# A later transposition of differences and of memory keys, and a softmax scaling that changes its engine

## The chip, the cores and the metric

The kernel runs on one core of one Trainium2 chip. The metric is the device time of one execution in microseconds (us). A core has TensorE (PE: products and transpositions; PEld are its weight loads), VectorE (DVE), ScalarE (ACT), GpSimd (POOL), SyncE (SP, which only issues transfers) and 16 DMA engines. Each engine does its own instructions in the order in which they were written; between engines there are only semaphores.

## The reference

Two layers of an encoder on 512 tokens of 1024 features, all in fp32. Layer 0 mixes tokens by dilated windows (8 heads, three dilations), layer 1 by grouped attention (8 query heads, 2 heads of keys and values). Both layers also attend to 256 memory tokens with 4 heads. The outputs are gated, projected and added to the residual stream:

```python
for i in range(DEPTH):
    h = rmsnorm(x, norm_g[i])
    mem_h = rmsnorm(mem, mem_norm_g[i])
    proj = jnp.einsum('bsd,de->bse', h, w_in_a[j])      # layer 1: w_in_b
    o_mix = mixer_dilated(qkv, ...)                     # layer 1: mixer_axial_gqa(q, k, v, ...)
    o_mem = memory_attention(q_mem, mem_h, w_mem_kv[i], mem_qn_g[i], mem_kn_g[i])
    y = jnp.concatenate([o_mix, o_mem], axis=-1) * jax.nn.silu(gate)
    x = x + jnp.einsum('bse,ed->bsd', y, w_out[i])

def memory_attention(q_mem, mem_h, w_kv, qn_g, kn_g):
    q = rmsnorm(q_mem, qn_g) * (HEAD_DIM ** -0.5)
    kv = mem_h @ w_kv                                   # keys (normed by heads) and values
    p = jax.nn.softmax(jnp.einsum('bqhe,bkhe->bhqk', q, k), axis=-1)
    return jnp.einsum('bhqk,bkhe->bqhe', p, v)
```

The grouped attention of layer 1 has the same softmax, over 512 keys.

## The kernel before

**Operands in two parts.** Each fp32 operand of a product is split into a high part (`wh`, or the first of a pair; a cast, mostly on ScalarE) and a low part (`wo`, the rest; a subtraction on VectorE). A product is then three matmuls, high by high, high by low and low by high: lines 163 to 165, `mm3`. For weights the cast is L285 and the subtraction L295.

**Products by Strassen's way.** The large projections (`s_chunk`, L352) use seven products instead of eight, and these need differences of halves of the rows and of the features. For layer 1 they are made from the rows that leave the first output projection. `ev_o` (L1187) takes one block b of 128 rows of the new x after the other: it stores it to DRAM, norms it, and for b = 2 and 3 calls `sum_h` (L504: S1, one subtraction on VectorE), waits `EO[2]` groups, and calls `sums_h` (L509), which transposes S1 (`put_h`: four transpositions into a bank `xT` on TensorE, then the split into `hS`, L157 and L160) and makes three more differences (L514 to L516). `rest_h` then transposes the others (S2, S4, S3, 22), one kind in each group. The tiles of the differences are called `xs` in the profile.

**Groups.** The `Driver` (L41) writes all engines' programs together. After each group of products (12 of 512 columns or 24 of 256) its `tick` lets every waiting generator do one step: `yield n` means go on after n groups. What is given to `drv.late` is written at the end of the tick, what is given to `drv.soon` at the start of the next. So a step's place in each engine's program is fixed by the number of groups, not by time. Where the program of TensorE has a transposition, its products behind it wait until the operand is there.

**Memory keys and values.** `mem_kv` (L593) projects the memory tokens in each layer, 48 products for keys and 48 for values. `ev_k` norms the keys (squares on ScalarE, `rstd` on GpSimd, the product `xn` on VectorE, L534), transposes them on TensorE (`qT`, L541) and splits them with their gain (`kmT`, L589 and L590). `ev_v` splits the values (`vm`, L607 and L609). In layer 1 this lies between the output projection of layer 0 and the first chunk of layer 1, right where `ev_o` ends. The products' banks `pj` are four, used in turn, so a bank of keys or values must be read before a later chunk writes it.

**Attention.** `mem_attn` (L629) and `attn_b` (L1314) are pipelines of steps over pieces of 256 queries (memory) or one head and 128 queries (grouped). In step t TensorE makes the scores of piece t (`sm`, `sb`), VectorE the row maximum (`top`, written late), ScalarE the exponentials of piece t - 1 with their row sums, VectorE for piece t - 2 the reciprocal of the row sum and the scaling of the probabilities by it and by 0.5 (L655; L1336), TensorE the transposition of piece t - 3 (`pmt`, `ptb`), ScalarE and VectorE its high and low part (`pmT`, `pbT`), and TensorE the product of piece t - 4 with the values (`om`, `ob`). The 0.5 belongs to the gate, which is made as t (1 + tanh(t / 2)). In layer 1 the probabilities `pb` take their tiles from the pool of 512-wide tiles that also holds the outputs `o` on their way to DRAM and `og` on their way back to the gates.

**GpSimd and the weights.** Sums of weight quarters are made by transfers that add (GpSimd issues them, lines 247 to 269). Its program also has the tables of layer 1 (L1223), which wait for `grB` on VectorE (L1220).

Of the kernel before, what the change touches and what calls it, by code (L numbers as in the profile page):

```python
# [10 lines left out]
F32 = mybir.dt.float32  # L11
F32R = mybir.dt.float32r
AF = mybir.ActivationFunctionType
ALU = mybir.AluOpType
# [12 lines left out]
MEM_STEP = 1, 1  # L27
MEM_D = 4
PD, W_EARLY = 1, True
EO = 1, 2, 1, 1, 1  # L30
YB = {"m": (2, 2), "k": (1, 1, 1), 0: (1, 2, 1), 1: (1, 2, 1)}
Y = [3, 2, 2, 2, 3, 2, 2, 1, 1, 1]

# [91 lines left out]
def trunk_kernel(ctx: ExitStack, tc: tile.TileContext, x, mem, wall, norm_g, mem_norm_g, gcol,  # L125
                 qn_a, kn_a, qn_b, kn_b, ident_d, mask_d, tab_a, tab_b, out):
    nc = tc.nc
    V, A, G, T = nc.vector, nc.scalar, nc.gpsimd, nc.tensor
# [14 lines left out]
    def s2(dt=F32, name="s2"):  # L143
        return pool.tile([128, 512], dt, tag="s2", name=name, bufs=NS2)
# [7 lines left out]
    def sm(n, name):  # L152
        return small.tile([128, n], F32, tag="sm%d" % n, name=name)
# [439 lines left out]
    def mem_kv(layer, M):  # L593
        kt_ = [m4(F32R, "kmT").rearrange("p (h t) -> p h t", h=4) for _ in range(2)]
        vt_ = [m4(F32R, "vm").rearrange("p (b e) -> p b e", b=2) for _ in range(2)]

        def ev_k(b, p):
            r = head_sq(p)
            yield 1
            xn = head_mul(p, r)  # L600
            yield 1
            q = transpose4(xn)
            cs = slice(b * 128, (b + 1) * 128)
            yield from put_norm(q, gk_m[layer], kt_[0][:, :, cs], kt_[1][:, :, cs])

        def ev_v(b, p):
            A.copy(vt_[0][:, b], p)  # L607
            yield 1
            V.tensor_tensor(vt_[1][:, b], p, vt_[0][:, b].bitcast(F32), ALU.subtract)  # L609

        proj_t(M, NAT[:2], ev_k)
        proj_t(M, NAT[:2], ev_v)
        return kt_, vt_
# [15 lines left out]
    def mem_attn(qm, km, vm, put, step):  # L629
# [8 lines left out]
                mm3(sp[:, j, :], qm[h // 2][0][:, h % 2, cs], qm[h // 2][1][:, h % 2, cs], km[0][:, h, :], km[1][:, h, :], True, True)  # L638

        def top(i):  # L640
            pr[i] = (sm(2, "nmm"), sm(2, "denm"), s2(name="pm").rearrange("p (b k) -> p b k", b=2))
            V.tensor_reduce(pr[i][0], sc[i], axis=AX.X, op=ALU.max, negate=True)

        def exps(i):
            nm, den, pp = pr[i]
            sp = sc.pop(i)
            for j in range(2):
                A.activation(pp[:, j], sp[:, j], AF.Exp, bias=nm[:, j:j + 1], accum_out=den[:, j:j + 1])

        def scale(i):  # L650
            _, den, pp = pr[i]
            rd = sm(2, "rdm")
            V.reciprocal(rd, den)
            for j in range(2):
                V.tensor_scalar(pp[:, j], pp[:, j], rd[:, j:j + 1], 0.5, ALU.mult, ALU.mult)  # L655

        def turn(i):
            pp = pr.pop(i)[2]
# [23 lines left out]
        def out_(i):  # L682
            h, b2 = divmod(i, 2)
            if b2:
# [2 lines left out]
                put(h, os)  # L687

        yield from pipeline(8, (0, score, 0), (4, pv, 0), (3, turn, 0), (2, scale, 0), (1, exps, 0),
                            (0, top, 1), (3, hi, 1), (3, lo, 1), (4, out_, 1), step=step)  # L690

    def out_rest(ys, acc, done, evac):

# [605 lines left out]
    def ev_kv(q, u, t):  # L1299
        i, j = int(q[0]) - 1, int(q[1]) - 1  # L1300
        if j:
            hi, lo = [v[:, 2 * i:2 * i + 2] for v in vb]
            tv = t.rearrange("p (b e) -> p b e", b=2)
            A.copy(hi, tv)
            yield 1
            V.tensor_tensor(lo, tv, hi.bitcast(F32), ALU.subtract)
# [7 lines left out]
    def attn_b():  # L1314
# [7 lines left out]
            mm3(sc[i], qh[h % 4 // 2][:, h % 2, cs], ql[h % 4 // 2][:, h % 2, cs], kbT[0][:, h // 4], kbT[1][:, h // 4], True, True)  # L1322

        def top(i):
            pr[i] = sm(1, "nmb"), sm(1, "denb"), s2(name="pb")
            V.tensor_reduce(pr[i][0], sc[i], axis=AX.X, op=ALU.max, negate=True)

        def exps(i):
            nm, den, pp = pr[i]
            A.activation(pp, sc.pop(i), AF.Exp, bias=nm, accum_out=den)  # L1330

        def scale(i):
            _, den, pp = pr[i]
            rd = sm(1, "rdb")
            V.reciprocal(rd, den)
            V.tensor_scalar(pp, pp, rd, 0.5, ALU.mult, ALU.mult)  # L1336

        def turn(i):
            b2, j = divmod(i, 2)
            pp = pr.pop(i)[2]  # L1340
            if j == 0:
                pts[b2] = [m4(F32R, "pbT").rearrange("p (k q) -> p k q", k=4) for _ in range(2)]
            tp[i] = at("ptb").rearrange("p (k q) -> p k q", k=4)
            for k in range(4):
                T.transpose(tp[i][:, k, :], pp[:, k * 128:(k + 1) * 128], ident)  # L1345
# [19 lines left out]
        def out_(i):  # L1365
# [5 lines left out]
            if b == 3:  # L1371
                put_ob(h, rs[h])

        yield from pipeline(32, (0, score, 0), (4, pv, 0), (3, turn, 0), (2, scale, 0), (1, exps, 0),
                            (0, top, 1), (3, hi, 1), (3, lo, 1), (4, out_, 1),
                            ready=lambda i: n_rot[0] >= 8 + i // 16 * 4)

    for kvh in range(2):
# [134 lines left out]
```

## Time and profile before

| | |
|---|---|
| median of 3 runs | 983.4 us (982.01 to 985.52) |
| profiled execution: its time | 983.15 us |
| profiled execution: its span, first to last instruction | 981.4 us |
| mean granted clock of TensorE | 0.995 |
| transpositions of differences, L471 | 48 instructions, TensorE idle 3.5 us ahead of them |
| transpositions of grouped probabilities, L1345 | 128 instructions, TensorE idle 2.5 us ahead of them |
| VectorE, scaling of probabilities | 32 of 128x512 (L1336), 32 of 128x256 (L655) |
| ScalarE, exponentials of grouped attention (L1330) | 32, 692 ns each |

TensorE is the engine to watch. Layer 0 ends near 660 us, where the output projection gives way to the memory projection of layer 1; the memory attention of layer 1 runs to about 785 us, the grouped attention from 786 to 945 us, under the projections and gates of layer 1. An engine's idle time is shown with what ended it. The end of a matmul is modelled: products that start 0.12 us apart are shown 0.28 us long, so a short wait can hide under the length of the product before it.

### The profile page before, as it was taken

To read this page: it belongs to the slowest core of one execution; us is meant where nothing else is said; L and a number is where in the kernel's file an instruction comes from. 1 tells how busy PE (TensorE), PEld (TensorE's weight loads), DVE (VectorE), ACT (ScalarE), POOL (GpSimd) and SP (SyncE) were. 2 spreads that over 40 slices of the span, in tenths; PEclk is the share of its full clock that TensorE was granted. 3 is DMA by queue.
4 is the path that set the end of the run, shared out by engine and by line. 5 is a ranking of instruction groups with operands and counts; after the bars stand their busy time and mean duration, and the time that the engine had idled before them with its cause. 6 is when DMAs were issued, how large, how long until landed. Compare 5 with 4: busy or idle time off the path is not lost.

```text
span 981.4 us, 16676 instructions
## 1 busy us (share of the span) xinstructions
PE 955.3 (97%) x5728; PEld 839.9 (86%) x5728; DVE 816.7 (83%) x1473; ACT 645.5 (66%) x1623; POOL 344.1 (35%) x484
## 2 busy tenths in 40 slices
PE   8999999999999999999999998998999999999898
PEld 5789888888888888888899986887999999998776
DVE  6997788878888888888888999778689998879873
ACT  5556668686767676768676665555677766566650
POOL 1122424656555555555544011323532321111001
PEclk9999999999999999999999999999999999999999
DMA  8979846869686868686949896979585877786544
GB/s 337 322 251 334 224 97 186 289 125 267 152 254 156 249 157 249 158 248 139 268 122 291 232 243 198 304 274 312 165 198 127 229 180 192 206 209 155 167 135 129
DMA packets 88982, 209.27 MB, mean 213 GB/s; under 512 B 25281, under 2 KB 36033, under 8 KB 88898
## 3 DMA queue, kind: packets, MB, share of 16 engines
q1 hardware_dynamic: 70034, 146.28, 43.1%
q0 software_dynamic: 17568, 59.78, 32.4%
q10 hardware_dynamic: 1296, 2.16, 0.6%
q8 instruction: 45, 0.74, 0.3%
q14 instruction: 39, 0.32, 0.1%
HBM read 157.79 MB, written 12.65 MB: 174 GB/s over the span
## 4 chain that ended last, share of the span: by engine, by line
PE 77%; DVE 12%; DMA 6%; ACT 2%; issue 2%; POOL 1%; SPq 0%; DVEq 0%; ACTq 0%; POOLq 0%
PE pj L163 20%; PE pj L165 20%; PE pj L164 20%; DVE wo L295 3%; PE qT L541 2%; DMA og<-od 2%; DMA odb<-o 2%; PE sa L1041 1%; PE oo L1143 1%; PE pt L1122 1%; PE sa L1037 1%; PE xT L471 1%; PE ptb L1345 1%; DMA og<-odb 1%; POOL tabs L1223 1%
## 5 line engine op out<-in xcount | busy, mean ns | idle before, releaser
L295 DVE TENSOR_TENSOR wo<-wl,wh 128x1024 fp32r<-128x1024 f32 x255 | 315.4, 1242 | 9.6 <-ACT wh L285 9.3
L285 ACT CAST wh<-wl 128x1024 fp32r<-128x1024 f32 x255 | 269.7, 1059 | 70.8 <-PE pj L165 36.1
L163 PE MATMUL pj<-wh,hS 128*128 128x512 f32 (+1 forms) x448 | 164.3, 367 | 0.1
L164 PE MATMUL pj<-wo,hS 128*128 128x512 f32 (+1 forms) x448 | 158.0, 353 | 1.4 <-DVE wo L295 1.4
L165 PE MATMUL pj<-wh,hS 128*128 128x512 f32 (+1 forms) x448 | 158.1, 353 | 0.0
L163 PE MATMUL pj<-wh,h 128*128 128x512 f32 (+1 forms) x336 | 124.0, 369 | 0.2 <-ACT h L157 0.2
L164 PE MATMUL pj<-wo,h 128*128 128x512 f32 (+1 forms) x336 | 119.3, 355 | 2.0 <-DVE wo L295 2.0
L165 PE MATMUL pj<-wh,h 128*128 128x512 f32 (+1 forms) x336 | 119.6, 356 | 0.0
L420 POOL TENSOR_TENSOR rstd<-mse,half 128x4 f32<-128x4 f32 (+2 forms) x98 | 98.4, 1005 | 8.2
L165 PEld LDWEIGHTS pj<-wh,hS 128*128 128x128 f32 x448 | 84.7, 189 | 12.3 <-DVE hS L160 0.2
L164 PEld LDWEIGHTS pj<-wo,hS 128*128 128x128 f32 x448 | 85.0, 190 | 11.9 <-DVE wo L295 2.0
L163 PEld LDWEIGHTS pj<-wh,hS 128*128 128x128 f32 x448 | 84.8, 189 | 10.1 <-ACT sn L360 0.3
L360 ACT COPY sn<-pj 128x512 f32<-128x512 f32 x132 | 73.7, 591 | 18.4 <-PE pj L165 15.3
L419 POOL TENSOR_SCALAR mse<-hss 128x4 f32<-128x4 f32 (+1 forms) x86 | 46.1, 536 | 110.5 <-ACT junk L529 103.5
L529 ACT ACTIVATE junk<-sn 128x128 f32<-128x128 f32 x264 | 79.0, 307 | 0.2 <-DVE sn L371 0.2
L985 POOL TENSOR_TENSOR ta<-sn,tabs 128x128 f32<-128x128 f32 (+1 forms) x64 | 37.0, 580 | 119.6 <-DVE sn L534 80.5
L164 PEld LDWEIGHTS pj<-wo,h 128*128 128x128 f32 x336 | 64.4, 192 | 9.7 <-DVE wo L295 2.3
L165 PEld LDWEIGHTS pj<-wh,h 128*128 128x128 f32 x336 | 64.1, 191 | 9.4 <-DVE h L160 0.2
L377 DVE TENSOR_TENSOR sn<-pj,sn 128x512 f32<-128x512 f32 x99 | 67.6, 684 | 4.8 <-PE pj L165 4.4
L163 PEld LDWEIGHTS pj<-wh,h 128*128 128x128 f32 x336 | 64.3, 191 | 7.7 <-ACT h L157 0.5
L269 POOL DMA_DIRECT2D wl<-wl x33 | 29.3, 888 | 111.2 <-DVE wo L295 61.0
L163 PE MATMUL pj<-hS,wh 128*128 128x256 f32 x192 | 55.9, 291 | 0.0
(229 smaller groups left out, 2461.4 us busy)
## 6 DMA issues: line engine op xcount, KB each, us to landing
wl<-in_wall_dram SPq DMA_DIRECT2D x222, 512.0 KB, 6.8
wl<-wl POOLq DMA_DIRECT2D x64, 512.0 KB, 5.5
wl<-in_wall_dram POOLq DMA_DIRECT2D x42, 512.0 KB, 8.4
acc<-sn POOLq DMA_DIRECT2D x16, 256.0 KB, 5.6
od<-o SPq DMA_DIRECT2D x12, 256.0 KB, 5.1
og<-od SPq DMA_DIRECT2D x12, 256.0 KB, 6.1
odb<-o SPq DMA_DIRECT2D x12, 256.0 KB, 3.6
og<-odb SPq DMA_DIRECT2D x12, 256.0 KB, 3.5
```

The source lines that it names most:

```text
L163: T.matmul(o, lh, rh, start=start, stop=False, skip_group_check=True)
L164: T.matmul(o, lh, rl, start=False, stop=False, skip_group_check=True)
L165: T.matmul(o, ll, rh, start=False, stop=stop, skip_group_check=True)
L269: G.dma_start(self.tile[key], self.tile[c, "T2", x], accum_op=ALU.add)
L285: A.copy(wh, self.tile[self.items[i]])
L295: V.tensor_tensor(wo, self.tile[key], wh.bitcast(F32), ALU.subtract)
L360: A.copy(t, b)
L377: V.tensor_tensor(t, b, t, ALU.subtract if q == "12" else ALU.add)
L419: G.tensor_scalar(e, ss, EPS, None, ALU.add)
L420: G.tensor_tensor(r, e, half[:, 0:n], ALU.pow)
L529: A.activation(jk, p[:, j * 128:(j + 1) * 128], AF.Square, scale=QS, accum_out=ss[:, j:j + 1])
L985: G.tensor_tensor(ta[:, 0:n], xn[:, 0:n, 0:32], ropeA[:, 0, b, s0:s0 + n], ALU.mult)
```

## The change

It has three parts.

1. `EO[2]` goes from 1 to 2: between `sum_h` and `sums_h` lie two groups instead of one. In `ev_k` both waits go from 1 to 2 groups, in both layers.
2. In both attentions the scaling of the probabilities moves from VectorE (`tensor_scalar` by the reciprocal and 0.5) to ScalarE (a copy with the reciprocal as its scale per row). The reciprocal is written one step earlier, at the end of step t for piece t - 1, right behind the row maximum of piece t.
3. The 0.5 moves to the values: their high part is a scaled copy on ScalarE, their low part a `scalar_tensor_tensor` on VectorE (memory values in both layers, grouped values in layer 1).

```diff
-EO = 1, 2, 1, 1, 1
+EO = 1, 2, 2, 1, 1
...
         def ev_k(b, p):
             r = head_sq(p)
-            yield 1
+            yield 2
             xn = head_mul(p, r)
-            yield 1
+            yield 2
             q = transpose4(xn)
...
         def ev_v(b, p):
-            A.copy(vt_[0][:, b], p)
+            A.activation(vt_[0][:, b], p, AF.Copy, scale=0.5)
             yield 1
-            V.tensor_tensor(vt_[1][:, b], p, vt_[0][:, b].bitcast(F32), ALU.subtract)
+            V.scalar_tensor_tensor(vt_[1][:, b], p, 0.5, vt_[0][:, b].bitcast(F32), ALU.mult, ALU.subtract)
...
         def exps(i):
-            nm, den, pp = pr[i]
+            nm, den, rd, pp = pr[i]
             A.activation(pp, sc.pop(i), AF.Exp, bias=nm, accum_out=den)
+        def recip(i):
+            V.reciprocal(pr[i][2], pr[i][1])
+
         def scale(i):
-            _, den, pp = pr[i]
-            rd = sm(1, "rdb")
-            V.reciprocal(rd, den)
-            V.tensor_scalar(pp, pp, rd, 0.5, ALU.mult, ALU.mult)
+            _, _, rd, pp = pr[i]
+            A.activation(pp, pp, AF.Copy, scale=rd)
...
         yield from pipeline(32, (0, score, 0), (4, pv, 0), (3, turn, 0), (2, scale, 0), (1, exps, 0),
-                            (0, top, 1), (3, hi, 1), (3, lo, 1), (4, out_, 1),
+                            (0, top, 1), (1, recip, 1), (3, hi, 1), (3, lo, 1), (4, out_, 1),
                             ready=lambda i: n_rot[0] >= 8 + i // 16 * 4)
```

`mem_attn` changes in the same way, with two halves of 256 columns to a piece; `ev_kv` changes as `ev_v` does. The new code is three lines longer, so its line numbers are two or three higher.

What moves on VectorE between the layers (near 664 us), from the first S1 difference on; `xs_7960` is the S1 difference of block 2, `hS` the low part of a transposed difference, `wo` a pair of weights' low parts, `xn` the normed keys. Before:

```order
L506 TENSOR_TENSOR xs_7960<-acc 128x512
L295 TENSOR_TENSOR wo<-wl,wh 128x1024 x2
L160 TENSOR_TENSOR hS_7997<-xT,hS_7997 128x4x128
L514 TENSOR_TENSOR xs_7995<-xs_7960,acc 128x512
L515 TENSOR_TENSOR acc<-acc 128x512
L516 TENSOR_TENSOR xs_7996<-acc,xs_7995 128x512
L506 TENSOR_TENSOR xs_8008<-acc 128x512
L534 TENSOR_TENSOR xn<-pj,rstd 128x512
```

And now:

```order
L506 TENSOR_TENSOR xs_7960<-acc 128x512
L295 TENSOR_TENSOR wo<-wl,wh 128x1024 x2
L506 TENSOR_TENSOR xs_7995<-acc 128x512
L160 TENSOR_TENSOR hS_8031<-xT,hS_8031 128x4x128
L514 TENSOR_TENSOR xs_8029<-xs_7960,acc 128x512
L515 TENSOR_TENSOR acc<-acc 128x512
L516 TENSOR_TENSOR xs_8030<-acc,xs_8029 128x512
L534 TENSOR_TENSOR xn<-pj,rstd 128x512
L295 TENSOR_TENSOR wo<-wl,wh 128x1024 x2
L160 TENSOR_TENSOR hS_8031<-xT,hS_8031 128x4x128
L514 TENSOR_TENSOR xs_8061<-xs_7995,acc 128x512
```

The S1 difference of block 3 (`xs_8008` before, `xs_7995` now) moves up, right behind the pair of weights; the next pair of weights moves up ahead of the second `hS`. On TensorE the transposition of `xs_7960` stood behind 24 products of the memory projection after the last rows of x (`acc`) and now stands behind 36; the two S1 transpositions have 12 products between them in both. Those of the keys (`qT`) stood with the second S1 transposition and with the S2 ones; now they stand with the S2 and the S4 ones. The last transpositions (`acc`, 22) stood behind the second group of the chunk that follows and now stand behind the third.

On VectorE in the grouped attention, at the step of 914 to 922 us, from the second gate product with attention outputs (`sn<-sn,og`) to the next weight. Before:

```order
L745 TENSOR_TENSOR sn<-sn,og 128x512 x2
L1335 RECIPROCAL rdb<-denb 128x1
L1336 TENSOR_SCALAR pb<-pb,rdb 128x512
L1326 TENSOR_REDUCE nmb<-sb 128x1
L1354 TENSOR_TENSOR pbT<-ptb,pbT 128x4x128
L377 TENSOR_TENSOR sn<-pj,sn 128x512
L295 TENSOR_TENSOR wo<-wl,wh 128x1024
```

And now:

```order
L747 TENSOR_TENSOR sn<-sn,og 128x512 x2
L1328 TENSOR_REDUCE nmb<-sb 128x1
L1335 RECIPROCAL rdb<-denb 128x1
L1357 TENSOR_TENSOR pbT<-ptb,pbT 128x4x128
L377 TENSOR_TENSOR sn<-pj,sn 128x512
L295 TENSOR_TENSOR wo<-wl,wh 128x1024
```

The scaling is gone from behind the gate product, and the reciprocal (of the piece one later) stands between the maximum and the low part. On ScalarE at the same place, from the weight's cast of that step (`yS` and `y` are high parts for the output projection, `pb,denb<-sb,nmb` the exponentials). Before:

```order
L285 CAST wh<-wl 128x1024
L1330 ACTIVATE pb,denb<-sb,nmb 128x512
L1349 CAST pbT<-ptb 128x4x128
L1370 COPY o<-ob 128x256
L285 CAST wh<-wl 128x1024
L769 CAST yS_11398<-yf 128x512 x2
L748 CAST y<-sn 128x2x256 x2
L1330 ACTIVATE pb,denb<-sb,nmb 128x512
```

And now:

```order
L285 CAST wh<-wl 128x1024
L1339 ACTIVATE pb<-pb,rdb 128x512
L1332 ACTIVATE pb,denb<-sb,nmb 128x512
L1352 CAST pbT<-ptb 128x4x128
L1373 COPY o<-ob 128x256
L285 CAST wh<-wl 128x1024
L771 CAST yS_11401<-yf 128x512 x2
L750 CAST y<-sn 128x2x256 x2
L1339 ACTIVATE pb<-pb,rdb 128x512
L1332 ACTIVATE pb,denb<-sb,nmb 128x512
```

Each step's scaling stands ahead of its exponential; the scaling of this step stands ahead of the casts of `y`, that of the next step behind them. The programs of GpSimd and SyncE are in the same order as before.

More of the change, by code (lines that the diff above doesn't have):

```diff
@@ L640, in top @@
         def top(i):
-            pr[i] = (sm(2, "nmm"), sm(2, "denm"), s2(name="pm").rearrange("p (b k) -> p b k", b=2))
+            pr[i] = (sm(2, "nmm"), sm(2, "denm"), sm(2, "rdm"), s2(name="pm").rearrange("p (b k) -> p b k", b=2))
             V.tensor_reduce(pr[i][0], sc[i], axis=AX.X, op=ALU.max, negate=True)
         def exps(i):
-            nm, den, pp = pr[i]
+            nm, den, rd, pp = pr[i]
             sp = sc.pop(i)
@@ L648, in exps @@
                 A.activation(pp[:, j], sp[:, j], AF.Exp, bias=nm[:, j:j + 1], accum_out=den[:, j:j + 1])
+        def recip(i):
+            V.reciprocal(pr[i][2], pr[i][1])
         def scale(i):
-            _, den, pp = pr[i]
-            rd = sm(2, "rdm")
-            V.reciprocal(rd, den)
+            _, _, rd, pp = pr[i]
             for j in range(2):
-                V.tensor_scalar(pp[:, j], pp[:, j], rd[:, j:j + 1], 0.5, ALU.mult, ALU.mult)
+                A.activation(pp[:, j], pp[:, j], AF.Copy, scale=rd[:, j:j + 1])
         def turn(i):
-            pp = pr.pop(i)[2]
+            pp = pr.pop(i)[3]
             pt2 = m4(F32R, "pmT").rearrange("p (a k q) -> p a k q", a=2, k=2)
@@ L689, in mem_attn @@
         yield from pipeline(8, (0, score, 0), (4, pv, 0), (3, turn, 0), (2, scale, 0), (1, exps, 0),
-                            (0, top, 1), (3, hi, 1), (3, lo, 1), (4, out_, 1), step=step)
+                            (0, top, 1), (1, recip, 1), (3, hi, 1), (3, lo, 1), (4, out_, 1), step=step)
     def out_rest(ys, acc, done, evac):
@@ L1303, in ev_kv @@
             tv = t.rearrange("p (b e) -> p b e", b=2)
-            A.copy(hi, tv)
+            A.activation(hi, tv, AF.Copy, scale=0.5)
             yield 1
-            V.tensor_tensor(lo, tv, hi.bitcast(F32), ALU.subtract)
+            V.scalar_tensor_tensor(lo, tv, 0.5, hi.bitcast(F32), ALU.mult, ALU.subtract)
         else:
@@ L1324, in top, with recip @@
         def top(i):
-            pr[i] = sm(1, "nmb"), sm(1, "denb"), s2(name="pb")
+            pr[i] = sm(1, "nmb"), sm(1, "denb"), sm(1, "rdb"), s2(name="pb")
             V.tensor_reduce(pr[i][0], sc[i], axis=AX.X, op=ALU.max, negate=True)
         def exps(i):
-            nm, den, pp = pr[i]
+            nm, den, rd, pp = pr[i]
             A.activation(pp, sc.pop(i), AF.Exp, bias=nm, accum_out=den)
+        def recip(i):
+            V.reciprocal(pr[i][2], pr[i][1])
         def scale(i):
-            _, den, pp = pr[i]
-            rd = sm(1, "rdb")
-            V.reciprocal(rd, den)
-            V.tensor_scalar(pp, pp, rd, 0.5, ALU.mult, ALU.mult)
+            _, _, rd, pp = pr[i]
+            A.activation(pp, pp, AF.Copy, scale=rd)
         def turn(i):
             b2, j = divmod(i, 2)
-            pp = pr.pop(i)[2]
+            pp = pr.pop(i)[3]
             if j == 0:
```

## The prediction

> **What bounds the kernel now.** I read the page first: the span, the busy shares and the chain that ended last.
>
> ```profile
> span 981.4 us, 16676 instructions
> PE 955.3 (97%) x5728; PEld 839.9 (86%) x5728; DVE 816.7 (83%) x1473; ACT 645.5 (66%) x1623; POOL 344.1 (35%) x484
> PE 77%; DVE 12%; DMA 6%; ACT 2%; issue 2%; POOL 1%; SPq 0%; DVEq 0%; ACTq 0%; POOLq 0%
> ```
>
> TensorE is the bound: busy for 955.3 of 981.4 us, and 77% of the chain. The change adds and removes no product, so it can pay only where TensorE waits, 26.1 us in all. The second view is what it waits for: waiter, releaser, us in all, times, longest.
>
> ```profile
> PE ob L164 <- DVE pbT L1354: 5.0, 3, 2.6
> PE xT L471 <- DVE xs L506: 3.5, 2, 1.9
> PE ptb L1345 <- ACT y L748: 1.8, 1, 1.8
> PE ptb L1345 <- DVE qb L1292: 0.4, 1, 0.4
> PE ptb L1345 <- DVE pbT L1354: 0.3, 1, 0.3
> ```
>
> These are the waits beside work that the change touches: the differences of rows (xs) between the layers, and grouped attention (ptb, pbT, ob). They are 11.0 us together. The third view puts them into stages: PE, PEld, DVE, ACT and POOL busy with their counts, the granted clock, the DMA share and GB/s.
>
> ```profile
> 660.00:680.00 20.00, 16.53 (x78) 12.90 (x77) 18.48 (x26) 9.96 (x28) 8.19 (x8) 0.91 1.04 334
> 780.00:800.00 20.00, 20.00 (x160) 19.43 (x159) 19.86 (x32) 15.64 (x46) 8.77 (x10) 1.00 0.92 253
> 800.00:820.00 20.00, 19.16 (x147) 17.61 (x147) 19.64 (x37) 10.59 (x20) 1.74 (x2) 1.00 0.58 139
> 880.00:900.00 20.00, 17.44 (x105) 15.79 (x104) 19.81 (x35) 13.48 (x26) 1.72 (x2) 0.91 0.64 159
> 920.00:940.00 20.00, 16.14 (x88) 13.56 (x89) 18.82 (x33) 12.42 (x24) 0.87 (x1) 1.00 0.49 149
> ```
>
> VectorE is nearly full in each of them and ScalarE has room. In two stages the granted clock is 0.91 as well, so a wait there costs more than its own length.
>
> **Part 1: the differences (EO), between the layers.** On TensorE, start, length and, in brackets, the idle time before:
>
> ```profile
> 657.66 0.40 PE L164 MATMUL pj<-wo,act 128*128 128x512 f32 x1
> 657.89 0.39 PE L165 MATMUL pj<-wh,act 128*128 128x512 f32 x1
> 664.87 0.63 PE L471 MATMUL xT<-ident,xs 128*128 128x128 f32 x4 [1.56 <-DVE xs L506]
> 670.14 0.63 PE L471 MATMUL xT<-ident,xs 128*128 128x128 f32 x4 [1.91 <-DVE xs L506]
> 672.29 0.63 PE L165 MATMUL pj<-wh,act 128*128 128x512 f32 x1
> 672.71 0.63 PE L163 MATMUL pj<-wh,act 128*128 128x512 f32 x1
> 687.13 1.04 PE L471 MATMUL xT<-ident,acc 128*128 128x128 f32 x8
> ```
>
> Products start 0.23 us apart (657.66, 657.89), after the second wait 0.42 apart (672.29, 672.71): half clock, as I read it for about 7 products, 7 x 0.2 = 1.4 us. With the two waits, 1.56 + 1.91 + 1.4 = 4.9 us are lost here. VectorE at the same place:
>
> ```profile
> 664.04 0.69 DVE L506 TENSOR_TENSOR xs<-acc 128x512 f32<-128x512 f32 x1
> 664.64 2.35 DVE L295 TENSOR_TENSOR wo<-wl,wh 128x1024 fp32r<-128x1024 f32 x2
> 666.91 0.68 DVE L160 TENSOR_TENSOR hS<-xT,hS 128x512 fp32r<-128x512 f32 x1
> 669.92 0.68 DVE L534 TENSOR_TENSOR xn<-pj,rstd 128x512 f32<-128x512 f32 x1
> ```
>
> In the new order the first transposition of a difference stands behind one more group of 12 products: TensorE reaches it at 664.87 - 1.56 + 12 x 0.23 = 666.1, and the difference is there at 664.7. That wait goes. The second is reached 0.4 (transposition) + 2.75 later, at 669.2; its difference now stands right behind the weight pair, 666.91 + 0.6 = 667.5 on VectorE. That wait goes too. Late next is the following pair, the S2 differences. VectorE has ahead of the second of them one hS, three subtractions, xn, a weight pair (now ahead of the second hS), hS and the difference itself: 7 x 0.60 + 2.27 = 6.5 us, so it is there at 674.0 to 674.1. TensorE comes at 669.2 + 0.4 + 2.75 + 0.4 = 672.7 and waits 1.4. The 1.56 wait did not bring the clock down and the 1.91 did, so I take full clock here. Gain at this place: 4.9 - 1.4 = 3.5 us.
>
> The rest of the step moves too. The two transpositions for the memory keys move one group, and the first V bank is read later: VectorE ends its vm at about 682.0, and the S1 products that write that bank start at about 683.1. No wait, with 1 us to spare. Does the gain last? The chain from here runs over GpSimd:
>
> ```profile
> 692.23 7.93 POOL tabs L1223 x4
> 706.81 7.87 DMA wl<-wl
> 717.50 0.48 ACT sn L360
> ```
>
> The tables on GpSimd (692.23) wait for VectorE's grB; rstd and a weight sum follow, whose transfer lands at 714.7; ScalarE then frees a bank at 718.0, just as TensorE comes to it. So TensorE gains only what grB gains. grB now follows the lows of the last transposition, which now stands one group (24 x 0.12 = 2.9 us) later: 687.13 - 3.5 + 2.9 = 686.5, plus 2.45 (687.13 to the end of these lows at 689.6 before) = 689.0 against 692.0. **Term 1: -3.1 us** (3.0 to 3.5, and 2.1 if the clock halves in the new wait: 3.5 - 1.4).
>
> **Part 2: the scaling moves to ScalarE.**
>
> ```profile
> L1336 DVE TENSOR_SCALAR pb<-pb,rdb 128x512 f32<-128x512 f32 x32 | 15.6, 487 | 1.1
> L655 DVE TENSOR_SCALAR pm<-pm,rdm 128x256 f32<-128x256 f32 x32 | 10.7, 377 | 0.6
> L732 ACT ACTIVATE th<-sn 128x512 f32<-128x512 f32 x24 | 15.3, 644 | 0.0
> L980 ACT COPY v<-sn 128x256 f32<-128x256 f32 x32 | 12.8, 399 | 0.0
> 899.50 1.16 ACT L732 ACTIVATE th<-sn 128x512 f32<-128x512 f32 x2
> ```
>
> VectorE loses 26.3 us of busy time; the reciprocals stay. No ScalarE scaling by a value per row from SBUF to SBUF is in the trace. Its bounds are the plain copy (128x256: 0.40) and the tanh (128x512: 0.64). Two tanhs in a row take 1.16, so one holds the engine 0.52 to 0.53; I take 0.53 for pb and 0.30 to 0.35 for pm. ScalarE gains 32 x 0.53 + 32 x 0.33 = 28 us. At 780 to 800 some 2.2 of that come to its 15.64 of 20, so PE's products still hide it; without that cover each would cost its 0.53. The 0.5 in the values' copies adds at most 0.1 us to six pieces each on ScalarE and VectorE, hidden; I take 0. The reciprocal now stands one step earlier, ahead of a low (pbT) on VectorE, and waits for ScalarE's exponential. Behind it stand that low and the next weights' lows. But the low waits for a cast that ScalarE does after that exponential, so it adds no wait. In the memory attention TensorE does not wait, so nothing is gained there.
>
> At 800 to 820 TensorE idles 0.84 us, in three short waits on VectorE. A product is shown 0.28 long at 0.12 apart, so each hides up to 0.16 more: 1.3 us. VectorE gets 0.40 a step back and comes earlier. **Term 2: -1.3** (0 to 1.4).
>
> The 2.6 us wait of ob (the longest of its row, at 882) hangs on VectorE's queue, where one scaling stood ahead of the low: **Term 3: -0.4** (0 to 0.6), and the lowered clock behind it stays.
>
> ```profile
> 912.95 0.69 ACT L1330 ACTIVATE pb<-sb,nmb 128x512 f32<-128x512 f32 x1
> 920.72 0.62 ACT L748 CAST y<-sn 128x512 fp32r<-128x512 f32 x1 [1.18 <-DVE sn L745]
> 920.00 0.69 DVE L745 TENSOR_TENSOR sn<-sn,og 128x512 f32<-128x512 f32 x1 [3.63 <-DMA og<-odb]
> 920.80 0.48 DVE L1336 TENSOR_SCALAR pb<-pb,rdb 128x512 f32<-128x512 f32 x1
> 926.52 0.68 DVE L1354 TENSOR_TENSOR pbT<-ptb,pbT 128x512 fp32r<-128x512 f32 x1
> ```
>
> At 916 to 920 VectorE stands behind a transfer (920.00), the scaling of 920.80 with it, and TensorE waits 1.8 us for that. On ScalarE the same scaling stands ahead of the exponential of 912.95, in front of the blocked cast, so this wait goes. But the next one, for the low of 926.52, hangs on the same transfer: VectorE starts at 920.00 as before and saves two scalings, 0.8 us. TensorE comes 2 us earlier and waits once, about 3.1 us (1.9 + 1.8 - 0.8 with the hidden parts), long enough to halve the clock: +1.4. The third wait (0.9, at 935) has gone by then, since VectorE has three scalings less. In all -0.8 + 1.4 - 0.9 = -0.3; without the half clock it is -0.8 and at 935 another -0.8, -1.6. **Term 4: -0.9**, the middle.
>
> **Sum.** -3.1 - 1.3 - 0.4 - 0.9 = -5.7 us. The profiled execution took 983.15 us (1.75 around its span); the median of the three runs is 983.4, a quarter of a us above, within their spread. 983.15 - 5.7 = 977.4.
>
> **The rivals.**
> (a) *The clock stays up in the attention.* Nothing halves at 882 and 926: -1.6 for -0.9 in term 4, and the part of the 0.91 at 880 to 900 comes back, 0.09 x 20 = 1.8: 977.4 - 0.7 - 1.8 = 974.9. For it: 1.8 us at 919 left the clock at 1.00. Against: 1.91 and 2.6 us did not. The Trainium skill ("TensorE: Matmul & The Clock Gate", section "What's actually happening") puts the half clock behind an idle window of about 3.4 us that runs freely; by that rule none of these waits must lower it, and the rows disagree, since 1.91 us did.
> (b) *Only the boundary pays.* Waits in the attention hang on transfers and casts, and a scaling less before them is idle time: -3.1, 980.0. The transfer in front of 920.00 speaks for it.
> (c) *The boundary wait only moves.* VectorE reaches the second S2 difference 2 us later than I sum, TensorE waits 3.4 us there and the clock halves again: term 1 is about 0, 980.5. The weight pair ahead of it speaks for this; the two waits that surely go speak against.
> (d) *Slower: ScalarE's queue sets the lows of grouped attention.* Each scaling stands ahead of the cast on which the low hangs, and in the 22 or so steps of 786 to 818 and 876 to 945, where VectorE now sets them, each would come 0.53 later: 22 x 0.53 = 11.7, less term 1: 983.15 + 8.6 = 991.8. It decides once ScalarE's work in a step exceeds the step's 4 us; with 15.64 + 2.2 of 20 it does not, unless its waits for others add up.
>
> **How the numbers follow.** Forecast 0.45; (a) 0.15; (b) 0.18; (c) 0.13; (d) 0.07; the 0.02 left is elsewhere. About 0.3%, 2.9 us, is what a measurement of this kernel can tell from no change, so faster means below 980.2. The forecast and (a) lie below, 0.60, and most of (b) and a third of (c): 0.75. Same: 0.18. Slower: 0.07, which is (d). Range: down to (a) with term 1 at its 3.5 and term 2 at 1.4, 974.4, put at 974.2; up to (c) with term 3 at zero, 980.9, put at 981.0.
>
> **What would show it.** Right: no wait of xT for L506 at 663 and 668, one of about 1.4 us for the S2 difference, clock 1.00 in that stage; grB some 3 us earlier; the wait of ptb at 919 gone and one longer wait of ob near 924; VectorE's busy time down by 26 us, ScalarE's up by 28 to 35. Wrong: a half clock behind the S2 difference; a new wait at the S1 products; lows of pbT that wait for ScalarE at 786 to 818; or ScalarE's scalings longer than 0.7 us.

## The result, and the profile after

The changed kernel takes 977.6 us (median of 6 runs, 975.42 to 978.92) against 983.03 us (981.15 to 985.52) of the kernel before beside it: a ratio of 0.9936, 95% interval 0.9914 to 0.9957, so 0.4 to 0.9% less. The forecast was 977.4. The total was right; three of its four terms were not, and their errors cancelled.

The page after, with the span, the busy shares and the chain that ended last (the profiled execution took 977.34 us):

```profile
span 975.5 us, 16658 instructions
PE 949.6 (97%) x5728; PEld 836.1 (86%) x5728; DVE 791.0 (81%) x1409; ACT 675.0 (69%) x1687; POOL 343.6 (35%) x484
PE 82%; DVE 6%; DMA 5%; ACT 3%; POOL 2%; issue 1%; SPq 0%; DVEq 0%; ACTq 0%; POOLq 0%
```

VectorE lost 25.7 us of busy time and ScalarE gained 29.5, as forecast; VectorE's part of the chain fell from 12% to 6%. TensorE's waits beside the changed work (waiter, releaser, us in all, times, longest; a fifth, at 709 us, follows with the stages):

```profile
PE ob L164 <- DVE pbT L1357: 2.6, 2, 1.5
PE xT L471 <- DVE hS L160: 1.5, 1, 1.5
PE xT L471 <- DVE xs L514: 1.4, 1, 1.4
PE pmt L666 <- ACT pm L649: 0.6, 1, 0.6
```

The waits of ptb are gone, those of ob are halved (5.0 to 2.6). The two waits for the S1 differences are gone, but two others of xT stand in their place: one was forecast (L514, the second S2 difference), one was not (hS). The fourth row is new as well and lies in layer 0. By stages, with the columns of before:

```profile
660.00:680.00 20.00, 17.99 (x102) 15.21 (x100) 16.58 (x22) 9.76 (x25) 9.57 (x8) 1.00 1.05 341
700.00:720.00 20.00, 18.21 (x153) 18.01 (x152) 14.28 (x18) 13.12 (x43) 12.53 (x16) 1.00 0.79 181
800.00:820.00 20.00, 20.00 (x161) 19.38 (x160) 17.75 (x33) 14.62 (x29) 2.07 (x3) 1.00 0.66 146
880.00:900.00 20.00, 18.27 (x111) 15.74 (x110) 19.97 (x35) 17.87 (x36) 3.15 (x4) 1.00 0.72 180
920.00:940.00 20.00, 18.85 (x108) 16.14 (x107) 18.15 (x28) 14.91 (x27) 1.61 (x2) 1.00 0.39 117
```

The clock is 1.00 at 660 and at 880, where it was 0.91. TensorE's products fill 800 to 820, and gain 2.7 us of busy time at 920 to 940. But at 700 to 720, where TensorE was full before (19.95 us busy), it now idles 1.8 us: the 1.5 us of busy time that 660 to 680 won are given back there. Some waits below (those of 1.77, 2.07, 2.99 and 3.08 us, and in the text those at 709 and 882) are counted from the spacing of the products, and come out up to 0.17 us longer than the idle time shown.

To compare kernels that enter a stage at different times, I cut TensorE's program at three of its instructions: the first product of layer 1's memory projection (647.50 us before), the first grouped score (786.19) and the last product (977.04). The lengths below are differences of these starts; beside them the number of places where the half clock followed a wait (1.6 to 1.8 us each: 3.41 us at half speed, last section).

| kernel | boundary and memory attention | half clocks | grouped attention to the end | half clocks |
|---|---|---|---|---|
| before | 138.7 | 1 | 190.9 | 1 |
| the change, profile of the result | 138.0 | 0 | 184.7 | 0 |
| the change, e5_full | 140.0 | 1 | 183.6 | 0 |
| the change, e12_full_again | 137.0 | 0 | 183.5 | 0 |
| e1_schedule_only | 137.8 | 0 | 189.5 | 1 |
| e2_scaling_only | 138.1 | 1 | 183.8 | 0 |
| e3_full_keys_early | 139.1 | 1 | 185.2 | 0 |
| e4_full_less_t2 | 135.3 | 0 | 183.6 | 0 |
| e6_grouped_only | 139.1 | 1 | 186.1 | 1 |
| e7_recip_early | 136.9 | 0 | 187.1 | 0 |
| e8_full_sum_on_gpsimd | 137.4 | 0 | 182.6 | 0 |
| e9_cast_behind | 135.2 | 0 | 184.7 | 0 |
| e10_two_casts_behind | 135.7 | 0 | 186.3 | 1 |
| e11_recip_late | 146.9 | 2 | 214.7 | 2 |

The forecast was -3.1 for the first stage and -2.6 for the second. The profile of the result shows -0.7 and -6.2. Each row is one execution, and the one of before has a half clock in both stages. Taken out at 1.7 us each, the first stage is 136.4 to 137.4 us in the four kernels with the old order (before, e2, e6, e7) and 137.0 to 138.3 in the four rows that have the whole new order and no other change there (the change three times, e1): the new order did not shorten it, and the -0.7 is the half clock that this execution did not have. In the second stage 187.8 to 189.2 (before, e1) stand against 182.6 to 185.2 in the ten rows with the scaling on ScalarE and the early reciprocal, 4 to 5 us less without any difference of the clock.

### The profile page after: what moved, and what is told of

Its sections match the earlier page's. It is cut to its first block, busy times and chain, and to the rows that moved or that the text cites. A ratio compares the mean times of both kernels' runs of the same rounds, so it can differ in the third digit from the quotient of the medians.

```text
span 975.5 us, 16658 instructions
## 1 busy us (share of the span) xinstructions
PE 949.6 (97%) x5728; PEld 836.1 (86%) x5728; DVE 791.0 (81%) x1409; ACT 675.0 (69%) x1687; POOL 343.6 (35%) x484
## 4 chain that ended last, share of the span: by engine, by line
PE 82%; DVE 6%; DMA 5%; ACT 3%; POOL 2%; issue 1%; SPq 0%; DVEq 0%; ACTq 0%; POOLq 0%
PE pj L163 21%; PE pj L165 21%; PE pj L164 21%; PE qT L541 2%; DMA og<-od 2%; PE sa L1043 1%; PE oo L1145 1%; DVE wo L295 1%; PE pt L1124 1%; PE sa L1039 1%; PE ptb L1348 1%; DMA odb<-o 1%; PE xT L471 1%; DMA wl<-wl 1%; DMA og<-odb 1%
## 5 line engine op out<-in xcount | busy, mean ns | idle before, releaser
L420 POOL TENSOR_TENSOR rstd<-mse,half 128x4 f32<-128x4 f32 (+2 forms) x98 | 101.8, 1039 | 8.2
L360 ACT COPY sn<-pj 128x512 f32<-128x512 f32 x132 | 73.8, 592 | 15.5 <-PE pj L165 11.8
L419 POOL TENSOR_SCALAR mse<-hss 128x4 f32<-128x4 f32 (+1 forms) x86 | 42.8, 498 | 115.2 <-ACT junk L529 111.3
```

The source lines that it names most:

```text
L360: A.copy(t, b)
L419: G.tensor_scalar(e, ss, EPS, None, ALU.add)
L420: G.tensor_tensor(r, e, half[:, 0:n], ALU.pow)
```

## The experiments

All ratios are to runs of the kernel before on the same chip in the same series, with 95% intervals.

### Which part pays

**e1_schedule_only**: the changed kernel without the scaling, that is `EO` and the two waits of `ev_k` alone.

```diff
-EO = 1, 2, 1, 1, 1
+EO = 1, 2, 2, 1, 1
...
-            yield 1
+            yield 2
```

> Only the waits change: two groups for the differences and for the memory keys; the scaling stays on VectorE with its 0.5. Theory A (formed from the profile after): the transfers that add up the first weights of layer 1 hold this place, and ScalarE, which waits for them, holds back the S2 splits, so the gain is about 1 us (0.5 to 1.5), 0.1%. Rival B (the terms on record): 3.1 us, 0.3%. Both expect the two waits of TensorE for the S1 differences gone; A expects a wait of about 1.5 us for a bank freed by VectorE's hS and a first wait of ScalarE for the weight sum of over 4 us near 675.

Measured: 1.0001 (0.9984 to 1.0017). The new order alone is worth nothing that can be measured: rival B's 0.3% lies outside the interval, theory A's 0.1% inside it. The wait of ScalarE that A expected is there, 5.10 us, before a cast at 677.64.

**e2_scaling_only**: the rest alone, with the order between the layers as before (`EO`, and the two waits of `ev_k` at 1).

```diff
-EO = 1, 2, 2, 1, 1
+EO = 1, 2, 1, 1, 1
```

> Only the scaling, the reciprocal's place and the 0.5 change; the waits for differences and keys are as before. A: nearly all of the gain, 4.5 to 5.5 us, 0.5%, and no half clock behind the ob wait near 880. B: 2.6 us, 0.27% (1.3 at 800 to 820, 0.4 at 882, 0.9 at 916 to 937), with the half clock still there.

Measured: 0.9968 (0.9953 to 0.9983), 3.1 us: B's size is inside the interval, A's (0.5%) at its edge. There is no half clock behind the wait of ob in its profile, as A expected. Its grouped stage is 7 us shorter than in the profile of before, but that one took 983.15 us, against a median of 980.8 for the kernel before in this series; the two profiles overstate the gain.

**e6_grouped_only**: scaling, reciprocal and the 0.5 changed in grouped attention alone.

> Scaling, earlier reciprocal and the 0.5 changed in grouped attention alone; memory attention and the order between the layers as before. Theory A: carries all of the gain of the scaling, ratio about 0.997 (0.9955 to 0.998), half clock behind the wait of ob at 882 gone, wait of ptb at 919 gone. Rival: half of VectorE's relief comes in the memory attention, and the ratio is 0.9985 or above.

Measured: 0.9943 (0.9924 to 0.9961), all of the gain. No gain of the memory attention shows in the times, and its traces have a small cost: the wait of pmt at 156 us, 0.59 us long, is in every profile with its scaling on ScalarE (2.09 us in e11_recip_late), and in no other.

**e5_full**: the changed kernel beside these.

> The changed kernel itself, timed beside the variants. Theory A (the scaling in grouped attention carries the gain; the boundary between the layers is held by a weight sum and gives little): ratio 0.9955 to 0.9970, 3 to 4.5 us below before. Theory of the prediction (the boundary pays 3 us and more): at least 2 us faster than the variant with the scaling alone, which had 0.9968, so a ratio of 0.9948 or less.

Measured: 0.9955 (0.9936 to 0.9975), no faster than e6_grouped_only. The expectation of the prediction (0.9948 or less, 2 us more than the scaling alone) is not met; its bound lies inside the interval, so it is e1_schedule_only that speaks against it.

### The reciprocal

**e7_recip_early**: the scaling stays on VectorE, but the reciprocal is written a step earlier, as in the change.

```diff
         def scale(i):
-            _, den, pp = pr[i]
-            rd = sm(1, "rdb")
-            V.reciprocal(rd, den)
+            _, _, rd, pp = pr[i]
             V.tensor_scalar(pp, pp, rd, 0.5, ALU.mult, ALU.mult)
...
-                            (0, top, 1), (3, hi, 1), (3, lo, 1), (4, out_, 1),
+                            (0, top, 1), (1, recip, 1), (3, hi, 1), (3, lo, 1), (4, out_, 1),
```

> Only the reciprocal written a step earlier; the scaling by it and by 0.5 stays on VectorE, the order between the layers is as before. Theory A (what pays is the scaling taken off VectorE's queue in front of the lows): ratio 0.999 to 1.000, the waits of ob at 882 (1.7 us and more) and of ptb at 919 stay. Rival (the order pays: the scaling no longer waits 0.19 us behind its reciprocal, and VectorE gets 0.1 us per piece): ratio 0.998 or less, half of what the scaling alone gave.

Measured: 0.9974 (0.9958 to 0.999): the rival holds in part. The order alone gives a gain, some 2.5 us. The waits that theory A named are still there, shorter: 1.68 us of idle time shown at 882 (2.56 before) and 1.40 at 917 (1.83). VectorE at the step of 916 us in this kernel:

```profile
917.14 0.69 DVE L1328 TENSOR_REDUCE nmb<-sb 128x1 f32<-128x512 f32 x1
917.74 0.15 DVE L1335 RECIPROCAL rdb<-denb 128x1 f32<-128x1 f32 x1
917.81 0.67 DVE L1357 TENSOR_TENSOR pbT<-ptb,pbT 128x512 fp32r<-128x512 f32 x1
```

The next instruction starts 0.07 us behind the reciprocal. Before, the scaling that reads it started 0.19 behind it (the prediction shows it, at 920.80; below are the instructions in front of and behind it):

```profile
920.61 0.16 DVE L1335 RECIPROCAL rdb<-denb 128x1 f32<-128x1 f32 x1
...
921.20 0.68 DVE L1326 TENSOR_REDUCE nmb<-sb 128x1 f32<-128x512 f32 x1
```

So a piece cost VectorE 0.59 us (920.61 to 921.20), and after the change 0.07: 0.52 less, not 0.40.

**e11_recip_late**: the changed kernel with the reciprocal put back to its old step, right ahead of ScalarE's scaling, in both attentions.

```diff
         def scale(i):
+            recip(i)
             _, _, rd, pp = pr[i]
             A.activation(pp, pp, AF.Copy, scale=rd)
...
-                            (0, top, 1), (1, recip, 1), (3, hi, 1), (3, lo, 1), (4, out_, 1),
+                            (0, top, 1), (3, hi, 1), (3, lo, 1), (4, out_, 1),
```

> The changed kernel with the reciprocal put back one step, where it was: ScalarE's scaling follows right behind it in the same step, so ScalarE waits for VectorE's queue. Theory A (taking the scaling off VectorE is the larger part, but only because the reciprocal is ready a step earlier): ScalarE waits 0.3 to 2 us in a step, its exponentials and casts come that much later, and the waits of ob at 882 and ptb at 919 come back in part: 1 to 4 us above the changed kernel. Rival (ScalarE has room in every step): within 1 us of the changed kernel. Slower rival (the waits add up, a us in each of 22 steps): 10 us and more above.

Measured: 1022.6 us, 1.0412 (1.0391 to 1.0432): 40 us slower than before, the slower rival. The waits of ScalarE and VectorE show it:

```profile
ACT pb L1341 <- DVE rdb L1336: 51.6, 31, 6.9
DVE pbT L1359 <- ACT pbT L1354: 50.5, 32, 3.1
...
ACT pm L658 <- DVE rdm L652: 24.4, 13, 3.6
```

With the change as it is, the first of them is small (the second is 13.2 us, and 11.8 before):

```profile
ACT pb L1339 <- DVE rdb L1335: 1.5, 2, 1.2
```

And this is how it closes on itself in one step of e11_recip_late, first on VectorE, then on ScalarE:

```profile
826.05 0.68 DVE L745 TENSOR_TENSOR yf<-sn,og 128x512 f32<-128x512 f32 x1
826.66 0.16 DVE L1336 RECIPROCAL rdb<-denb 128x1 f32<-128x1 f32 x1
...
829.66 0.69 DVE L1359 TENSOR_TENSOR pbT<-ptb,pbT 128x512 fp32r<-128x512 f32 x1 [2.26 <-ACT pbT L1354]
```

```profile
826.91 0.72 ACT L1341 ACTIVATE pb<-pb,rdb 128x512 f32<-128x512 f32 x1 [2.95 <-DVE rdb L1336]
827.53 0.67 ACT L1333 ACTIVATE pb<-sb,nmb 128x512 f32<-128x512 f32 x1
...
829.04 0.59 ACT L1354 CAST pbT<-ptb 128x512 fp32r<-128x512 f32 x1 [0.27 <-PE ptb L1350]
```

The reciprocal stands behind VectorE's other work of the step. ScalarE waits 2.95 us for it with the exponential and the cast queued behind; then VectorE waits 2.26 us for that cast. Each in-order engine waits once a step for the other. Written a step earlier, the reciprocal is there before ScalarE comes to it. Without that placement the change is a loss.

### The boundary between the layers

ScalarE after the change, ahead of the unforeseen wait of xT (that for hS, at 679):

```profile
671.83 1.06 ACT L285 CAST wh<-wl 128x1024 fp32r<-128x1024 f32 x1 [0.81 <-PE pj L165]
678.65 1.05 ACT L285 CAST wh<-wl 128x1024 fp32r<-128x1024 f32 x1 [5.77 <-DMA wl<-wl]
679.61 1.07 ACT L157 CAST hS<-xT 128x512 fp32r<-128x512 f32 x2
```

A weight's cast stands 5.77 us in the queue, waiting for a transfer that adds two weight quarters; the casts of the differences transposed at 673 and 675 stand behind it, their lows on VectorE behind them, and a transposition on TensorE, at 680.97, waits 1.54 us for a bank. In the kernel before the same cast stood behind those of the differences, and did not wait for the transfer:

```profile
676.19 1.07 ACT L157 CAST hS<-xT 128x512 fp32r<-128x512 f32 x2 [3.83 <-PE xT L471]
679.84 1.05 ACT L285 CAST wh<-wl 128x1024 fp32r<-128x1024 f32 x1 [0.33 <-PE pj L165]
```

(In the other two profiles of the change the transfer came 0.1 and 1.7 us sooner, counted from the first cut, the wait for a bank was below 0.8 us, and the one at 709 was 2.6 instead of 1.9.) GpSimd's tables wait for grB, which VectorE makes at the end of all this; after the change:

```profile
691.53 0.21 DVE L1222 TENSOR_SCALAR grB<-grB 128x128 f32<-128x128 f32 x1
```

**e3_full_keys_early**: the change, with the two waits of `ev_k` as before.

```diff
-            yield 2
+            yield 1
```

> The whole change, but the memory keys are transposed as early as before. If the keys' place is of no account (A and B): within 0.7 us of the changed kernel, about 977.6. Rival C: an early transposition of keys puts a wait for xn between the S1 transpositions and costs 1 to 2 us, 979.

Measured: 0.9958 (0.9944 to 0.9973), no difference. The wait for xn that rival C named came, 2.99 us at the keys' transposition at 666, but in the place of the two waits of xT and not on top of them, so its 1 to 2 us did not. A wait of 2.07 at 709 halved the clock.

**e4_full_less_t2**: the change without the sum of T1 into T2 for the first chunk of layer 1 (that addition is left out).

```diff
-                    if c:
+                    if c == 20:
+                        pass
+                    elif c:
```

> The whole change; left out is one addition of the weights of layer 1's first chunk (T1 into T2, a transfer of 512 KB that adds), so one product of seven has a wrong weight. A: ScalarE's 5.8 us wait for that sum near 678 goes, the S2 splits come some 4 us earlier, TensorE's 1.5 us wait for a bank at 679 goes and the tables on GpSimd start 1.5 us or more earlier: 1.5 to 2.5 us faster than the changed kernel, 975.3 to 976.1. B: VectorE's order alone sets this place and the sum is not waited for: 977.6.

Measured: 972.75 us, 0.991 (0.9894 to 0.9926). The first stage is 3.4 us shorter than before, and 2.7 shorter than in the profile of the change. The gain is larger than the 1.5 to 2.5 us of theory A. The kernel also moves 512 KB less, so this run alone doesn't tell whether the transfer itself or the cast that waits for it holds the stage; e9_cast_behind does.

**e8_full_sum_on_gpsimd**: that sum as an addition on GpSimd.

```diff
+                    if c == 20:
+                        G.tensor_tensor(self.tile[key], self.tile[key], self.tile[c, "T1", x], ALU.add)
+                    elif c:
```

> The changed kernel, with the second weight sum (T1 into T2) of layer 1's first chunk done by additions on GpSimd instead of adding transfers. Theory A (ScalarE stands 5.8 us behind that transfer near 678, its casts of the differences and TensorE's bank behind it): the wait of xT at 679 goes, TensorE reaches the memory attention 1 to 3 us earlier, total 1 to 3 us below the changed kernel (972.75 was measured with the sum left out). Rival 1 (GpSimd is slower at it, or its tables come later): the wait at 679 or the one at 709 grows, and the total is the same or up to 3 us longer.

Measured: 0.9947 (0.9924 to 0.997), not separate from the change. A wait of 2.91 us for a difference, at 676, took the place of the two (rival 1). That is 1.47 us more than the 1.44 of the change, and 1.47 us is what a subtraction on VectorE took too long, 2.15 instead of 0.68 (last section); VectorE did not idle from there to the difference.

**e9_cast_behind**: the change, with that one cast written behind the casts of differences, values and keys. The sum itself is as in the change.

```diff
-... self.ripe(self.at, self.items[i], force, 1 if ... else None):
+... self.ripe(self.at, self.items[i], force, 1 if ... else 4 if self.items[i][:2] == (20, "T2") else None):
```

> The changed kernel, with one cast of ScalarE written later: the high part of the weight sum (T2) of layer 1's first chunk now stands behind the two casts of differences, a cast of values and one of keys, instead of ahead of them. Theory A (what holds the boundary near 679 is ScalarE standing in its order behind that transfer): ScalarE casts the differences at about 676 instead of 679.6, the 1.7 us wait of xT at 679 goes, TensorE starts the second chunk of differences 1.5 us earlier; of that 0 to 1.5 us last, since the next weight sum (709) still sets the end of this stage: total 0 to 1.5 us below the changed kernel. Rival (VectorE's own queue frees that bank late): the wait at 679 stays at 1 us or more. Rival 2 (the weight is now late for its products near 690): a new wait there, total up to 3 us longer.

Measured: 974.34 us, 0.9922 (0.9902 to 0.9942); the change in the same series 976.06. That is the lowest of the kernels that do the whole computation, but the two intervals overlap, so the total is not shown to be shorter. The first stage is as short as with the sum left out, 135.2 us against 137.0 to 140.0 in the three profiles of the change. On ScalarE:

```profile
675.29 0.59 ACT L157 CAST hS<-xT 128x512 fp32r<-128x512 f32 x1 [1.49 <-PE xT L471]
675.77 0.60 ACT L608 ACTIVATE vm<-pj 128x512 fp32r<-128x512 f32 x1
676.26 0.69 ACT L589 ACTIVATE kmT<-qT,gc 128x512 fp32r<-128x512 f32 x1
678.40 1.05 ACT L285 CAST wh<-wl 128x1024 fp32r<-128x1024 f32 x1 [1.45 <-DMA wl<-wl]
```

The transfer lands as late as before (0.3 us later, counted from the first cut), but no cast of a difference stands behind it: the differences are cast as soon as TensorE has transposed them, the wait at 679 is gone, and grB is early:

```profile
688.79 0.22 DVE L1222 TENSOR_SCALAR grB<-grB 128x128 f32<-128x128 f32 x1
```

The forecast for it was 689.0. With that one cast moved, and the transfer as it was, the stage is 1.8 us or more shorter: the cast's place in ScalarE's order is the cause.

**e10_two_casts_behind**: the same for the second chunk's cast too.

```diff
-... else 4 if self.items[i][:2] == (20, "T2") else None):
+... else 4 if self.items[i][0] in (20, 21) and self.items[i][1] == "T2" else None):
```

> As the run before, and the same for the second chunk: its T2 cast stands behind the copy of a projection (sn) that frees a bank, instead of ahead of it. Theory A: the wait at 709 (1.9 to 2.6 us in profiles of the changed kernel) goes to 0.7 or less, since that copy no longer stands 6 us behind a transfer; the boundary is then worth the forecast 3 us, and the total is 2 to 3.5 us below the changed kernel (ratio to before 0.992 to 0.994). Rival (the bank waits for VectorE, or the weights are late for their products): the wait at 709 stays, or turns up near 716, and the total is that of the run before.

Measured: 0.9939 (0.9921 to 0.9957); the first stage is as with e9_cast_behind. The wait at 709 stays at 0.92 us, now for a weight's low part: the rival. The further 2 us that theory A expected did not come.

### The same kernel again, and the clock

**e12_full_again**: the changed kernel once more.

> The changed kernel once more, beside the three variants of this call and with a third profile. Ratio 0.994 to 0.997. If the half clock behind a wait is chance at a given length (the untouched wait of 1.77 us near 598 was followed by it in five of ten profiles), this profile differs from the other two of the same kernel by about 1.6 us at each wait of 1.7 us and more where the clock falls or doesn't; waits below 1.5 us never lower it.

Measured: 0.9937 (0.9915 to 0.9959), a little below the 0.994 expected. At 598 us lies a wait of 1.77 us that no variant touches. Over the 14 profiles of this case it brought the half clock 7 times and stayed without it 7 times. Two profiles of the same changed kernel there, each in two steps of 3.41 us, this run's first, then the result's (PE, PEld, DVE, ACT, POOL busy, clock, DMA share, GB/s):

```profile
598.89:602.30 3.41, 1.36 (x11) 0.94 (x9) 3.41 (x9) 1.95 (x4) 0.34 (x1) 1.00 0.80 167
602.30:605.71 3.41, 3.41 (x10) 2.68 (x9) 3.41 (x6) 1.81 (x3) 0.00 (x0) 0.50 1.04 284
```

```profile
597.76:601.17 3.41, 1.76 (x7) 1.18 (x7) 3.41 (x7) 1.65 (x3) 0.86 (x1) 1.00 0.82 159
601.17:604.59 3.42, 2.96 (x17) 2.48 (x17) 3.42 (x8) 2.11 (x4) 0.00 (x0) 1.00 0.80 201
```

One has the half clock, for the whole step behind the wait, and the other not. The last section says why the steps are cut there.

## Why the prediction was right, and where it wasn't

**Term 1 (boundary, -3.1): wrong, it was near 0 (e1_schedule_only), and the -0.7 of the profile is a half clock that did not come.** The steps on TensorE and VectorE held: both waits for S1 went, the wait for the second S2 difference was 1.44 us against 1.4, at full clock, and the S1 products did not wait for the V bank. What failed first is the step that put the lows of the last transposition at 689.0. It followed only TensorE and VectorE, and left out ScalarE's queue: in the new order a weight's cast stands ahead of the differences' casts, and its operand lands only at 678.6. So grB came at 691.5 instead of 689.0. The second step that failed is "TensorE gains only what grB gains": what was left went at 709, where the next chunk's cast waits 6.09 us in the same way. The transfer that it waits for took 5.75 us from issue to landing, against 4.66 before; issued 1.2 us earlier, counted from the first cut, it landed 0.1 us earlier. In e12_full_again grB came as early as forecast by that count (41.4 us behind the first cut; 689.0 is 41.5), this transfer took 6.4 us, and the stage was no shorter than the old order without a half clock. Why the transfer takes longer was not tried. e9_cast_behind shows the cause of the first: without that one cast in front the stage is 2.8 us shorter than in the profile of the change (3.4 than before, a half clock of that), grB is at 688.8, and the wait at 709 is down to 1.0 us. The forecast -3.1 is the size of a boundary that the change alone does not reach. The outcome resembles rival (c), but by another mechanism: VectorE did not come late, ScalarE did.

**Term 2 (800 to 820, -1.3): right.** All three waits went. Counted from the first grouped score, TensorE's scores come 1.6 us earlier behind this part.

**Term 3 (ob at 882, -0.4): too small, -2.1.** The wait itself shrank by about 0.6 us: it was 2.72 in one piece, and is now 0.42 and, one product later, 1.73:

```profile
881.11 0.39 PE L163 MATMUL ob<-pbT,vb 128*128 128x256 f32 x1 [0.26 <-ACT pbT L1352]
882.96 0.39 PE L164 MATMUL ob<-pbT,vb 128*128 128x256 f32 x1 [1.47 <-DVE pbT L1357]
```

The step "the lowered clock behind it stays" failed: 1.6 us more. That is rival (a)'s clock at 882. That it stayed up in this execution is in part luck: with the scaling moved the second piece was 1.44 to 1.84 us and lowered the clock in two of ten profiles, and in the kernels with the scaling on VectorE the wait (1.84 to 2.72) lowered it in two of three.

**Term 4 (916 to 937, -0.9): too small, about -2.8.** The wait of ptb went as forecast, and that at 935. The one wait of ob that remains is 1.15 us, not 3.1, and leaves the clock up:

```profile
922.11 0.39 PE L164 MATMUL ob<-pbT,vb 128*128 128x256 f32 x1 [1.15 <-DVE pbT L1357]
```

The step that failed is "VectorE starts at 920.00 as before". VectorE after the change, behind the same transfer:

```profile
915.91 0.69 DVE L747 TENSOR_TENSOR sn<-sn,og 128x512 f32<-128x512 f32 x1 [2.93 <-DMA og<-odb]
```

Counted from the first grouped score, that is 129.4 us against 133.8 before. The transfer was not a fixed point: the outputs that it carries were made earlier, and the store that puts them into DRAM (odb) was issued 3.7 us earlier by the same count (118.65 against 122.31), which is what TensorE had gained by then. The store also landed 0.6 us sooner behind its issue.

**Part 2, the prices.** ScalarE's scaling was dearer than the 0.53 us that I took from the tanhs, and VectorE's relief larger than 0.40 (0.52). The groups after:

```profile
L1339 ACT ACTIVATE pb<-pb,rdb 128x512 f32<-128x512 f32 x32 | 23.5, 734 | 1.6 <-DVE rdb L1335 1.5
L657 ACT ACTIVATE pm<-pm,rdm 128x256 f32<-128x256 f32 x32 | 14.6, 510 | 0.0
L1335 DVE RECIPROCAL rdb<-denb 128x1 f32<-128x1 f32 x32 | 4.9, 153 | 3.1 <-ACT pb L1332 3.1
```

It is shown 0.73 us long, above the 0.7 that the prediction named as a sign of being wrong; the next instruction starts 0.62 behind it (826.91 to 827.53 above). The Trainium skill ("ScalarE: Activation LUTs", section "What ACT_TABLE_LOAD costs") gives 0.186 us, 0.093 for an operand per row and 0.833 ns an element, less 0.093 of overlap: an estimate of 0.61 by that page, and the rows agree. ScalarE's queue, at 17.87 of 20 us in 880 to 900, still carried it, so that sign was set too low. The lows of pbT hardly waited for ScalarE at 786 to 818: 0.3 us once, 0.2 before.

**The reciprocal.** The prediction gave its move no price ("it adds no wait"). True of the wait, but it missed that the move is worth a gain by itself (e7_recip_early) and that without it the change loses 40 us (e11_recip_late). Rival (d) came nearest to this, in its last clause ("unless its waits for others add up"), and priced a step at 0.53; e11_recip_late shows 51.6 us of waits in 31 steps, 1.7 us each, since the two queues wait for each other.

So 977.4 came out by luck, by errors that cancel: +2.4 us in the first stage (-0.7 for -3.1), -3.6 in the second (-6.2 for -2.6, of which 1.7 is the half clock at 882), and the 1.0 us by which this execution was late at the first cut. Part of that 1.0 is the new wait of pmt at 156 us (0.59), a cost of the moved scaling in the memory attention of layer 0 that the prediction did not have; the rest was not followed. That the attention carries the gain and the order between the layers none of it rests on e1_schedule_only and e6_grouped_only, not on these two profiles.

## What to carry to other kernels

When work moves to another in-order engine, ask first where its operand is written: written one step ahead, the moved scaling cost its 0.62 us of an engine that had room; written in the same step, it made two queues wait for each other in 31 of 32 steps. Follow a moved tile through every engine that touches it, including the one with room: what stands ahead of it there may be waiting for a transfer. And a transfer that ends a wait is no fixed point in time if its source is made on the path that gets shorter.

## What the runs showed of the hardware that was not expected

**The half clock hangs on where a wait falls.** The unchanged wait of 1.77 us at 598 brought it in 7 of 14 profiles; in the stages of the table it came behind 1.73 us (e6_grouped_only) and stayed away behind 3.08 (e8_full_sum_on_gpsimd). No wait below 1.73 us brought it. The traces show an order in this. A half clock lasts 3.41 us, and where a profile has several, they start a whole number of 3.413 us apart (before: 670.97 and 886.01, 63 steps). So each profile can be cut into steps of 3.413 us. From 40 us to the last product, every step at full clock in which TensorE is shown busy for 1.60 us or less was followed by a step at half clock (20 in the 14 profiles), none with more than 1.75 was, and between the two bounds one of six. (In the opening, near 22 us, three profiles stayed at full clock behind 1.48 to 1.58.) The wait in e8_full_sum_on_gpsimd lies across two such steps, with 2.24 and 1.66 us busy; the two pairs of steps at 598 above show one case on each side. Three profiles of the same changed kernel differ at 598, so to the author of an edit the place of a step is chance: a profile with one half clock more or less differs by 1.6 to 1.8 us without any cause in the kernel. The Trainium skill ("TensorE: Matmul & The Clock Gate", section "What's actually happening") has a window of about 3.4 us that runs freely, and the half clock behind at least one idle window. The steps fit the first; the second does not fit, since a step with 1.5 us of products was enough.

**A VectorE subtraction ran three times as long beside an addition on GpSimd.** In e8_full_sum_on_gpsimd, GpSimd and then VectorE:

```profile
670.07 3.67 POOL L257 TENSOR_TENSOR wl<-wl 128x1024 f32<-128x1024 f32 x1 [2.70 <-DMA wl<-in_wall_dram]
```

```profile
671.54 0.69 DVE L160 TENSOR_TENSOR hS<-xT,hS 128x512 fp32r<-128x512 f32 x1
672.14 2.15 DVE L516 TENSOR_TENSOR xs<-xs,acc 128x512 f32<-128x512 f32 x1
674.22 0.68 DVE L517 TENSOR_TENSOR acc<-acc 128x512 f32<-128x512 f32 x1
```

The subtraction of two tiles in SBUF (L516) ends 0.55 us behind the addition's end at 673.74 and takes 2.15 us; that of a bank and a tile (L160) took its usual 0.69 beside the addition. It is not the only case: in the kernel before, beside the tables on GpSimd (692.23 to 700.16), the two `wo` subtractions from 692.05 on took 3.46 us, where the pair at 664.64 took 2.35. What holds it there, no run here tries.
